# Neighbourhood attention: the two end half blocks of keys as one stacked block of 128 rows

## The chip, the cores and the metric

One core of a Trainium2 chip runs the whole kernel. The metric is the time of one execution on the device in microseconds (us); the time before is 2090.88 us, the median of three runs (2089.56 to 2090.99). The engines are called PE (TensorE, matmul), PEld (its weight load), DVE (VectorE), ACT (ScalarE), POOL (GpSimd) and SP (SyncE, which issues the transfers).

## The reference, cut to what matters

The kernel computes one inference step of a two-layer backbone for 128 context tokens and 512 latent tokens. The latent tokens form a grid of 8 rows and 64 columns. The changed part is the attention of the odd layer for the latent tokens, eight heads of width 128. Each query reads all 8 grid rows, but only a window of 16 columns, and all 128 cached context keys:

```python
s_nb = einsum('brqhd,brkwhd->brhqkw', qg, kg) * scale      # qg: queries, kg: keys of the neighbourhood
s_nb = where(col_ok, s_nb + bias, NEG)                      # learned bias by offset, NEG outside the window
s_ctx = einsum('brqhd,blhd->brhql', qg, ck) * scale         # cached context keys
p = softmax(concatenate([s_nb, s_ctx], -1), -1)
o = einsum('brhqkw,brkwhd->brqhd', pn, vg) + einsum('brhql,blhd->brqhd', pc, cv)
```

`pn` and `pc` are the two parts of `p`. Context tokens attend among themselves without a window. All of it is in 32-bit floats.

## The kernel before, in words

The projections of both layers are long streams of matmuls with 128 x 128 weight blocks. Each weight is split into a high part (`whi`, by ACT) and a low part (`wlo`, by POOL), and each activation into `acth` and `actl`, so that three fast passes (320 or 322 columns) stand for one in full precision. The odd layer's projections are done in pairs of chunks by a Strassen scheme (`spair`), whose combined weights DVE makes.

The attention heads are coroutines that run between those matmuls. The whole program is written out by a planner: class `Pace` (line 53) keeps a modelled clock for each engine, and with it the time at which each piece of a buffer becomes ready. Between two products of the weight stream `tick` lets the waiting coroutines go on, if their inputs are ready by the model (`until`, `bank`, `calm`). So the order of instructions on every engine is fixed at build time, and it follows from the modelled costs. On the chip an engine works through its own list in order; semaphores hold it back where an operand isn't there yet.

`na_head` (line 2056) is one head. The latent tokens are reordered so that eight groups of 8 columns follow one another, each of them with its 8 rows: 64 positions a group, 512 in all. The queries go in four blocks of 128 (two groups each), and a fifth block holds the context tokens' queries. The keys that the four blocks need, with the window of 16 columns, are cut at `edges` into five pieces: 64, 128, 128, 128 and 64 positions. Query block b reads pieces b and b + 1, so the first and the last half piece serve one block each (0 and 3), and each of the three full pieces serves two.

A head goes as follows.

1. The values are transposed by PE to have positions in rows: the context's 128 and the three full pieces into one PSUM bank, copied by ACT to `vk[:, 0:512]`; then the two half pieces (64 rows each) into a second bank, copied by one ACT instruction to `vk[:64, 512:768]`.
2. `blocks` (line 1662) runs the five query blocks in a software pipeline of three steps. `s1` multiplies queries with keys and adds the bias (DVE) and takes the exponential (ACT). `soft2` divides by the sum (DVE). `s3` transposes the probabilities (PE, three transposes for a latent block: two pieces and the context) and copies them from PSUM to `pT`: two DVE copies of 128 columns for the pieces, and one ACT copy for the context. A half piece has 64 rows there.
3. The final product sums everything into one bank `po` of 512 columns, in one accumulation group: the context part (128 contraction rows, 512 columns), the first half piece (64 rows, 128 columns), the three full pieces (128 rows, 256 columns each), the last half piece (64 rows, 128 columns). ACT copies `po` to the head's output rows, and a transfer takes them to DRAM.

All matmuls and transposes of a head are in 32-bit floats; one of them shows as two passes in the trace. The buffers `bm`, `vk`, `pT`, `nk` and four `pieces` lie in the memory of `Y`, which held the gating branch's normalised values until then; `open_na` (line 2538) lays them out when that branch's last products have been put in order before it.

Of the kernel before, what the change touches and what calls it, by code (L numbers as in the profile page):

```python
# [13 lines left out]
AF = mybir.ActivationFunctionType  # L14
# [227 lines left out]
class Trunk:  # L242
# [1813 lines left out]
    def na_head(self, h, q, k, vt):  # L2056
        nc, L = self.nc, self.L
        Yh = vt
        kl, ql, vl = k[:, NCTX:T], q[:, NCTX:T], vt[:, NCTX:T]
        if h:  # L2060
            yield from self.wait(f"nh{h - 1}")
        bm, nk = L["bm"], L["nk"].next()
        self.dma(bm, self.d["na_bias"][h])
        self.dma(nk[:, 0:128], self.d["cache_na_kT"][h])
        self.dma(nk[:, 128:256], self.d["cache_na_v"][h])

        spec = [(0, 3, 0), (1, 4, 320), (3, 4, 320), (5, 3, 704)]

        vk = L["vk"]
        edges = [(0, 64), (64, 192), (192, 320), (320, 448), (448, 512)]  # L2070
        yield from self.until(vt)
        pv = self.sm()
        self.tr(pv[:, 0:128], vt[:, 0:NCTX])
        for i in (1, 2, 3):
            a, e = edges[i]
            self.tr(pv[:, 128 * i : 128 * i + 128], vl[:, a:e])
        nc.scalar.activation(vk[:, 0:512], pv, AF.Copy)
        pv = self.sm()
        for i, t in ((0, 0), (1, 4)):
            a, e = edges[t]  # L2080
            self.tr(pv[:64, 128 * i : 128 * i + 128], vl[:, a:e])
        nc.scalar.activation(vk[:64, 512:768], pv[:64, 0:256], AF.Copy)
        vkt = [vk[:64, 512:640], vk[:, 128:256], vk[:, 256:384], vk[:, 384:512], vk[:64, 640:768]]
        self.flags.add(f"nv{h}")
        yield from self.until(bm, nk)
        pT = L["pT"]

        slot = {(0, 0): 768, (0, 1): 0, (1, 1): 128, (1, 2): 256, (2, 2): 384, (2, 3): 512, (3, 3): 640, (3, 4): 896}
        info = {}

        def s1(t, p):
            info[t] = p
            ps = self.sm()
            if t == 0:
                self.mm(ps[:, 0:128], q[:, 0:NCTX], k[:, 0:NCTX])
                return self.soft1(p, ps, bm[:, 192:320], 128, None)
            g0, n, off = spec[t - 1]
            n *= 64
            qs = ql[:, 128 * (t - 1) : 128 * t]
            self.mm(ps[:, 0:n], qs, kl[:, 64 * g0 : 64 * g0 + n])  # L2100
            self.mm(ps[:, n : n + 128], qs, nk[:, 0:128])
            return self.soft1(p, ps, bm[:, off : off + n + 128], n + 128, None)

        def s3(t):
            p = info[t]
            pt = self.sm()
            if t == 0:
                self.tr(pt[:, 0:128], p[:, 0:128])
                nc.vector.tensor_copy(p[:, 128:256], pt[:, 0:128])
                return  # L2110
            b = t - 1
            g0, n, off = spec[b]
            n *= 64
            for i, j in enumerate((b, b + 1)):
                a, e = edges[j]
                self.tr(pt[: e - a, 128 + 128 * i : 256 + 128 * i], p[:, a - 64 * g0 : e - 64 * g0])
            self.tr(pt[:, 0:128], p[:, n : n + 128])
            for i, j in enumerate((b, b + 1)):
                m = edges[j][1] - edges[j][0]
                s = slot[(b, j)]  # L2120
                nc.vector.tensor_copy(pT[:m, s : s + 128], pt[:m, 128 + 128 * i : 256 + 128 * i])
            nc.scalar.activation(pT[:, 1024 + 128 * b : 1152 + 128 * b], pt[:, 0:128], AF.Copy)
            if t == 1:
                po = self.sm()
                self.mm(po[:, 0:128], vk[:, 0:128], info[0][:, 128:256])
                nc.scalar.activation(Yh[:, 0:NCTX], po[:, 0:128], AF.Copy)

        yield from self.blocks(5, s1, s3, 2, ())
        self.flags.add(f"nq{h}")
        yield from self.until(pT)  # L2130
        po = self.sm()
        self.mm(po, nk[:, 128:256], pT[:, 1024:1536], stop=False)
        self.mm(po[:, 0:128], vkt[0], pT[:64, 768:896], start=False, stop=False)
        for j in (1, 2, 3):
            self.mm(po[:, 128 * (j - 1) : 128 * (j + 1)], vkt[j], pT[:, 256 * (j - 1) : 256 * j], start=False, stop=False)
        self.mm(po[:, 384:512], vkt[4], pT[:64, 896:1024], start=False, stop=True)
        y4 = Yh[:, NCTX:T].rearrange("p (r g c) -> p g r c", g=8, c=8)
        o4 = po.rearrange("p (g r c) -> p g r c", r=8, c=8)
        nc.scalar.activation(y4, o4, AF.Copy)
        self.dma(self.ysp[:, h, :], vt)  # L2140
        self.flags.add(f"nh{h}")
        yield
# [54 lines left out]
    def program(self):  # L2197
        nc, tc, d, Y = self.nc, self.tc, self.d, self.Y
# [95 lines left out]
        for h in range(4):  # L2294
# [18 lines left out]
            p = (f"gla_elem{h - 1}",) if h else ()  # L2313
# [57 lines left out]
        for kv in range(2):  # L2371
# [26 lines left out]
            for h in range(4 * kv, 4 * kv + 4):  # L2398
                if kv and h != 5:
                    i = max(h - 5, 0)  # L2400
# [137 lines left out]
        def open_na():  # L2538
            S = self.slots
            L["hq"], L["hk"], L["nv"] = (Ring([S[n] for n in x]) for x in ("AB", "CD", "ER"))  # L2540
            more = Y.rearrange("p a b -> p (a b)")
            at = [0]

            def yt(n):
                at[0] += n
                return more[:, at[0] - n : at[0]]

            L["bm"], L["vk"], L["pT"] = yt(1024), yt(768), yt(1536)
            L["nk"] = Ring([yt(256), self.wraws[:, 1792:2048]])
            self.pieces = [yt(384) for _ in range(4)]  # L2550

        do(open_na)
        for h in range(8):

# [61 lines left out]
        r = acts.pop()  # L2616
# [271 lines left out]
```

## Time and profile before

| | |
|---|---|
| median of three runs | 2090.88 us |
| the profiled execution, its own time | 2094.82 us |
| its span, first to last instruction | 2093.0 us |
| instructions in the span | 40200 |
| PE, PEld busy | 98%, 95% |
| DVE, ACT, POOL busy | 63%, 51%, 61% |
| mean granted TensorE clock | 0.996 |

The span is what the trace covers; the profiled execution's own time has a little around it. "Busy" counts the records of an engine, and PE's records overlap, since a matmul begins while the one before it is still draining; a full PE is therefore not the same as a PE at its best pace. The helpers that record every instruction for the planner have one line for all of them (L215 for DVE, ACT and POOL, L400 for matmuls, L405 for transposes), so groups are told apart by the buffers they write and read, and by form. "128*128 128x256" is a matmul with a stationary block of 128 rows and 128 columns, and a moving operand of 128 rows and 256 columns.

### The profile page before, as it was taken

The numbers are of one execution on the slowest core, as the hardware profiler recorded it, in microseconds if no ns is written. First come the engines' busy times: TensorE is split into PE (matmuls) and PEld (weight loads), VectorE is DVE, ScalarE is ACT, GpSimd is POOL, SyncE is SP. The second block draws the span as 40 slices with busy tenths as digits, with TensorE's granted clock in tenths as the row PEclk, the third lists the DMA queues.
The fourth block names the chain that finished last, engine by engine and source line by source line (L and its number), as shares of the span: only waits on it lengthen the run. The fifth ranks groups of instructions, "written<-read, shape, count | busy, mean of one in ns | idle before, by whom it ended". The sixth has DMA issues, their size and how long they took to land. (4 is left out here: it accounts for less than half of the span.)

```text
span 2093.0 us, 40200 instructions
## 1 busy us (share of the span) xinstructions
PE 2047.3 (98%) x14345; PEld 1995.9 (95%) x14345; DVE 1327.3 (63%) x3070; ACT 1064.4 (51%) x2446; POOL 1275.1 (61%) x1072
## 2 busy tenths in 40 slices
PE   7999999999999999999999999999999999999997
PEld 6889999999999999999999999999999999999997
DVE  4757677676555655788786878787454554456444
ACT  5545555445665765444564434444444554454443
POOL 4655454445545554788765666655555577768884
PEclk9999999999999999999999999999999999999998
DMA  9956333436456444577734454454322334363427
GB/s 367 396 195 205 124 122 110 142 112 188 153 170 190 142 137 148 167 222 226 249 131 135 136 159 153 139 156 139 98 86 95 95 129 135 112 235 121 139 90 251
DMA packets 192697, 340.18 MB, mean 163 GB/s; under 512 B 20752, under 2 KB 70000, under 8 KB 192496
## 3 DMA queue, kind: packets, MB, share of 16 engines
q1 hardware_dynamic: 191296, 336.45, 49.7%
q8 instruction: 112, 1.84, 0.4%
q10 hardware_dynamic: 1200, 1.17, 0.2%
q14 instruction: 89, 0.73, 0.1%
HBM read 303.03 MB, written 31.88 MB: 160 GB/s over the span
## 5 line engine op out<-in xcount | busy, mean ns | idle before, releaser
L400 PE MATMUL bank<-acth,whi 128*128 128x320 f32 (+3 forms) x3320 | 1017.7, 317 | 4.7 <-ACT YB L215 1.4
L400 PE MATMUL bank<-acth,wlo 128*128 128x320 f32 (+3 forms) x3320 | 991.7, 310 | 0.9 <-POOL wlo L215 0.9
L400 PE MATMUL bank<-actl,whi 128*128 128x320 f32 (+3 forms) x3320 | 991.5, 310 | 0.0
L215 POOL TENSOR_TENSOR wlo<-wraw,whi 128x512 fp32r<-128x512 f32 (+1 forms) x446 | 568.1, 1285 | 439.1 <-ACT whi L215 368.4
L400 PEld LDWEIGHTS bank<-acth,whi 128*128 128x128 f32 (+1 forms) x3320 | 614.9, 188 | 12.5 <-issue 3.0
L400 PEld LDWEIGHTS bank<-actl,whi 128*128 128x128 f32 (+1 forms) x3320 | 615.5, 188 | 1.7
L400 PEld LDWEIGHTS bank<-acth,wlo 128*128 128x128 f32 (+1 forms) x3320 | 614.1, 188 | 1.9 <-POOL wlo L215 1.9
L215 POOL TENSOR_TENSOR wlo<-rs,whi 128x384 fp32r<-128x384 f32 x370 | 407.9, 1120 | 205.6 <-ACT whi L215 173.2
L215 ACT ACTIVATE whi<-wraw 128x512 fp32r<-128x512 f32 (+1 forms) x456 | 261.3, 588 | 126.7 <-PE bank L400 85.7
L215 ACT ACTIVATE whi<-rs 128x384 fp32r<-128x384 f32 x370 | 184.4, 518 | 83.2 <-PE bank L400 69.1
L400 PE MATMUL bank<-eh,whi 128*128 128x322 f32 (+1 forms) x666 | 208.9, 314 | 1.0 <-ACT whi L215 1.0
L400 PE MATMUL bank<-eh,wlo 128*128 128x322 f32 (+1 forms) x666 | 206.8, 310 | 1.2 <-POOL wlo L215 0.9
L400 PE MATMUL bank<-el,whi 128*128 128x322 f32 (+1 forms) x666 | 206.3, 310 | 0.0
L215 DVE CUSTOM_DVE_ANT_0 adas<-adas,bank,partg 128x256 bf16<-128x256 f32 (+1 forms) x296 | 160.6, 543 | 15.6 <-DMA adas<-ada_g 8.0
L215 DVE TENSOR_TENSOR wraw<-rs 128x768 f32<-128x768 f32 x74 | 98.8, 1335 | 100.7 <-DMA rs<-w_odd 55.4
L215 POOL TENSOR_TENSOR prod<-adas,mixrow 128x512 f32<-128x512 f32 x76 | 99.4, 1317 | 68.5 <-ACT prod L215 47.9
L215 ACT ACTIVATE arena<-arena,bc 128x512 f32<-128x512 f32 (+4 forms) x189 | 97.8, 538 | 78.6 <-DVE arena L215 73.7
L400 PEld LDWEIGHTS bank<-eh,wlo 128*128 128x128 f32 x666 | 125.1, 188 | 2.4 <-POOL wlo L215 2.4
L400 PEld LDWEIGHTS bank<-eh,whi 128*128 128x128 f32 x666 | 125.4, 188 | 1.3 <-ACT whi L215 1.2
L400 PEld LDWEIGHTS bank<-el,whi 128*128 128x128 f32 x666 | 125.4, 188 | 0.0
L215 DVE CUSTOM_DVE_ANT_0 adas<-adas,bank,part 128x512 bf16<-128x512 f32 x150 | 111.6, 744 | 19.6 <-DMA adas<-ada 16.7
L215 DVE TENSOR_TENSOR bank<-bank,sums 128x320 f32<-128x320 f32 (+1 forms) x148 | 70.8, 493 | 82.5 <-PE bank L400 61.3
(226 smaller groups left out, 2458.9 us busy)
## 6 DMA issues: line engine op xcount, KB each, us to landing
wraw<-w_even SPq DMA_DIRECT2D x176, 256.0 KB, 3.4
adas<-ada_g SPq DMA_DIRECT2D x128, 256.0 KB, 3.7
adas<-ada SPq DMA_DIRECT2D x128, 256.0 KB, 3.7
rs<-w_odd SPq DMA_DIRECT2D x50, 384.0 KB, 3.3
wraw<-w_odd SPq DMA_DIRECT2D x74, 256.0 KB, 3.6
wraw<-w_out SPq DMA_DIRECT2D x60, 256.0 KB, 3.9
rs<-w_odd SPq DMA_DIRECT2D x50, 256.0 KB, 3.8
Y<-ada SPq DMA_DIRECT2D x24, 512.0 KB, 7.8
```

The source lines that it names most:

```text
L215: return f(*args, **kw)
L400: self.nc.tensor.matmul(out, lhsT, rhs, start=start, stop=stop, **kw)
```

## The change

The two half pieces are laid above each other as one block of 128 rows: the first piece's 64 rows stay in rows 0 to 63, the last piece's go to rows 64 to 127.

- Values: the first half piece is transposed as before. For the last one, 128 positions (384 to 511) are transposed, so that its 64 land in rows 64 to 127. ACT copies the two halves with two instructions into one block `vk[:, 512:640]`.
- Probabilities: the last block's transpose takes 64 columns more (`lead`), so that its half piece lands in rows 64 to 127 too, and the copy takes those rows. The other rows of the two strips of `pT` are filled with zeros once, by POOL in `open_na`.
- Copies: for the two middle query blocks, whose two pieces lie side by side in `pT`, DVE makes one copy of 256 columns in place of two of 128.
- Product: one matmul of 128 rows and 256 columns takes the place of the two of 64 rows and 128 columns. Its output is two strips of `po`, columns 0 to 127 and 384 to 511. It stands last in the group; the first half piece's product stood second.
- `vk` is 128 columns shorter, and the buffers behind it move up.

```diff
@@ na_head: values
-        for i, t in ((0, 0), (1, 4)):
-            a, e = edges[t]
-            self.tr(pv[:64, 128 * i : 128 * i + 128], vl[:, a:e])
-        nc.scalar.activation(vk[:64, 512:768], pv[:64, 0:256], AF.Copy)
-        vkt = [vk[:64, 512:640], vk[:, 128:256], vk[:, 256:384], vk[:, 384:512], vk[:64, 640:768]]
+        self.tr(pv[:64, 0:128], vl[:, 0:64])
+        self.tr(pv[:, 128:256], vl[:, 384:512])
+        nc.scalar.activation(vk[:64, 512:640], pv[:64, 0:128], AF.Copy)
+        nc.scalar.activation(vk[64:, 512:640], pv[64:, 128:256], AF.Copy)
...
+        lead = {(3, 4): 64}
@@ s3
                 a, e = edges[j]
+                a -= lead.get((b, j), 0)
                 self.tr(pt[: e - a, 128 + 128 * i : 256 + 128 * i], p[:, a - 64 * g0 : e - 64 * g0])
...
-            for i, j in enumerate((b, b + 1)):
-                m = edges[j][1] - edges[j][0]
-                s = slot[(b, j)]
-                nc.vector.tensor_copy(pT[:m, s : s + 128], pt[:m, 128 + 128 * i : 256 + 128 * i])
+            if b in (1, 2):
+                s = slot[(b, b)]
+                nc.vector.tensor_copy(pT[:, s : s + 256], pt[:, 128:384])
+            else:
+                for i, j in enumerate((b, b + 1)):
+                    o = lead.get((b, j), 0)
+                    r, s = slice(o, o + edges[j][1] - edges[j][0]), slot[(b, j)]
+                    nc.vector.tensor_copy(pT[r, s : s + 128], pt[r, 128 + 128 * i : 256 + 128 * i])
@@ final product
         self.mm(po, nk[:, 128:256], pT[:, 1024:1536], stop=False)
-        self.mm(po[:, 0:128], vkt[0], pT[:64, 768:896], start=False, stop=False)
         for j in (1, 2, 3):
-            self.mm(po[:, 128 * (j - 1) : 128 * (j + 1)], vkt[j], pT[:, 256 * (j - 1) : 256 * j], start=False, stop=False)
-        self.mm(po[:, 384:512], vkt[4], pT[:64, 896:1024], start=False, stop=True)
+            self.mm(po[:, 128 * (j - 1) : 128 * (j + 1)], vk[:, 128 * j : 128 * j + 128], pT[:, 256 * (j - 1) : 256 * j], start=False, stop=False)
+        ends = po.rearrange("p (a b) -> p a b", b=128)[:, 0:4:3, :]
+        self.mm(ends, vk[:, 512:640], pT[:, 768:1024].rearrange("p (a b) -> p a b", b=128), start=False, stop=True)
@@ open_na
-            L["bm"], L["vk"], L["pT"] = yt(1024), yt(768), yt(1536)
+            L["bm"], L["vk"], L["pT"] = yt(1024), yt(640), yt(1536)
...
+            nc.gpsimd.memset(L["pT"][64:, 768:896], 0.0)
+            nc.gpsimd.memset(L["pT"][:64, 896:1024], 0.0)
```

## The prediction

> **What bounds the kernel now.** I read the page first, then the busy time by stretches, then the chain of waits, and last the order of TensorE's instructions inside the changed stage. A word on measure: 0.2% of 2090.9 us is 4.2 us, and a difference below that can't be told from no change here.
>
> ```profile
> span 2093.0 us, 40200 instructions
> ...
> PE 2047.3 (98%) x14345; PEld 1995.9 (95%) x14345; DVE 1327.3 (63%) x3070; ACT 1064.4 (51%) x2446; POOL 1275.1 (61%) x1072
> ```
>
> TensorE (PE) is busy 98% of the span, no other engine above 63%. The changed code runs where the eight attention heads of the odd layer run, about 1330 to 1700 us. These are that stretch and the one behind it; the columns are the window, its length, then busy us and instruction counts of PE, PEld, DVE, ACT and POOL, then the granted clock and DMA:
>
> ```profile
> 1330.00:1700.00 370.00, 370.00 (x2464) 356.81 (x2463) 220.39 (x653) 181.34 (x453) 208.43 (x188) 1.00 0.37 114
> 1700.00:2050.00 350.00, 350.00 (x2381) 349.95 (x2380) 172.63 (x265) 160.20 (x349) 269.46 (x234) 1.00 0.43 139
> ```
>
> PE is busy all 370 and all 350 us, at full granted clock; the others have 40% or more free in the first stretch. The chain of waits that ended last says the same: from the end of the last head's blocks it is one unbroken run of matmuls (start, length, engine, count):
>
> ```profile
> 1681.37 387.59 PE bank L400 x2602
> ```
>
> So PE time taken out of a head is end-to-end time, as long as PE's operands stay early. But "busy" is not "streaming": the record of a matmul spans its waiting for weights as well. What a matmul costs is read from start to start.
>
> **The change, part by part.** *The final product.* These are PE's rows of one head's last product (the second head), single instructions from narrow windows of the timeline: start, length, form as rows*columns of the stationary block, then the moving one. An fp32 matmul shows as two passes.
>
> ```profile
> 1400.51 0.30 PE L400 MATMUL bank<-eh,whi 128*128 128x322 f32 x1
> ...
> 1400.95 1.02 PE L400 MATMUL bank<-Y,wraw 128*128 128x512 f32 x2
> 1401.38 0.59 PE L400 MATMUL bank<-Y,wraw 128*128 128x512 f32 x1
> 1401.91 0.37 PE L400 MATMUL bank<-Y 64*128 64x128 f32 x1
> 1402.12 0.27 PE L400 MATMUL bank<-Y 64*128 64x128 f32 x1
> 1402.32 0.48 PE L400 MATMUL bank<-Y 128*128 128x256 f32 x1
> 1402.64 0.38 PE L400 MATMUL bank<-Y 128*128 128x256 f32 x1
> 1402.86 0.38 PE L400 MATMUL bank<-Y 128*128 128x256 f32 x1
> ...
> 1403.50 0.38 PE L400 MATMUL bank<-Y 128*128 128x256 f32 x1
> 1403.81 0.37 PE L400 MATMUL bank<-Y 64*128 64x128 f32 x1
> 1404.03 0.27 PE L400 MATMUL bank<-Y 64*128 64x128 f32 x1
> 1404.23 0.41 PE L400 MATMUL bank<-acth,whi 128*128 128x322 f32 x1
> 1404.48 0.31 PE L400 MATMUL bank<-actl,whi 128*128 128x322 f32 x1
> ```
>
> The steady paces: a 512-column pass 1401.38 - 1400.95 = 0.43 us; a 256-column pass (1403.50 - 1402.64) / 4 = 0.215, four steps because three passes lie between; a 322-column weight pass (1400.95 - 1400.51) / 3 = 0.147. By column that is 0.84 ns for fp32, so 128 columns would be 0.107.
>
> The 64-row passes don't keep that pace. The 512's second pass should be through at 1401.38 + 0.43 = 1401.81, but the 64-row one starts at 1401.91: 0.10 lost. Its second pass follows after 0.21 where 0.107 would do: 0.10. The 256 comes 0.20 behind that: 0.09. The second 256 pass comes 0.32 behind the first, where 0.215 is the pace: 0.105. So one half block costs four exposed steps, about 0.40 us beside its 0.215 of streaming. The second half block, from 1403.50, repeats it: 0.31 to the first pass (0.095 lost), 0.22 (0.11), 0.20 (0.09), and 0.25 to the second weight pass (0.10). Why it is exposed stands in the weight-load rows:
>
> ```profile
> 1401.90 1.58 PEld L400 LDWEIGHTS bank<-Y 64*128 64x128 f32 x8 [0.76 <-issue]
> 1403.81 0.29 PEld L400 LDWEIGHTS bank<-Y 64*128 64x128 f32 x2 [0.33 <-DVE arena L215]
> ```
>
> The weight loader, which elsewhere runs one pass ahead of the matmuls, stood idle 0.76 and 0.33 us and loads the 64-row block only when the pass before has run out. The releaser of the second (a DVE work on another buffer) is only the last semaphore that the profile found; both places look alike, so I take it as a drain at the change of block height, not as a wait for data.
>
> Stacked, there is no 64-row pass left. The new sequence is 512 columns (2 x 0.43), then four products of 256 columns (8 x 0.215), then the weight stream. From the first 512 pass to the second weight pass it should last 0.86 + 1.72 + 0.15 = 2.73 us. Before, it lasts 1404.48 - 1400.95 = 3.53 here, and as much in the first and the last head:
>
> ```profile
> 1357.03 3.34 PE L400 MATMUL bank<-Y 128*128 128x512 f32 x12
> ...
> 1360.55 0.31 PE L400 MATMUL bank<-actl,whi 128*128 128x320 f32 x1
> 1689.23 1.02 PE L400 MATMUL bank<-Y,wraw 128*128 128x512 f32 x2
> ...
> 1692.75 0.31 PE L400 MATMUL bank<-actl,whi 128*128 128x322 f32 x1
> ```
>
> 1360.55 - 1357.03 = 3.52 and 1692.75 - 1689.23 = 3.52. Gain: 3.52 - 2.73 = 0.79 us a head. All 32 such passes (8 heads, 4 each) show it in one group of weight loads (count, busy us, mean ns, idle us before them):
>
> ```profile
> L400 PEld LDWEIGHTS bank<-Y 64*128 64x128 f32 x32 | 4.7, 184 | 8.7 <-issue 7.4 <-DVE partg L215 0.7 <-DVE arena L215 0.3
> ```
>
> So 8 x 0.79 = **6.3 us off PE**. What the trace doesn't show is a product written in two strips of one bank, 384 columns apart. From below: the pace of the contiguous 256 (0.215 a pass). From above: each of its passes pays an exposed step as the 64-row ones do, on either side, 2 x 0.105 a head more, so 0.58 a head and 4.6 us in all. I take the first, since the form (128 rows, 128 columns, 256 moving, a contiguous moving operand) is that of the three products ahead of it, which already write at different places of the same bank without loss. The zeros cost nothing of their own: the 256 columns stream either way.
>
> A rule of the Trainium skill speaks against all this. "TensorE: Matmul & The Clock Gate" says, in the table of "Why this matters for your kernels", that a product with few contraction rows takes the time of one with 128, and in "Back-to-back issue gap" it counts columns only; by that, two products of 128 columns and one of 256 cost alike, and the sum is nothing. The trace differs: 0.61 us for a half block where its columns are worth 0.215. "TensorEngine Tiling (Array Packing)", "Key Properties", has the rule that would join the two: changing the tiling mode drains the engine. The rows above look like that.
>
> *The transposes.* Two of each head's 64-wide ones become 128 wide (one of values, one of probabilities, the last block's); the count stays. A trio of the last block (full, half, context) beside a trio of full blocks:
>
> ```profile
> 1354.93 0.49 PE L405 MATMUL bank<-ident,Y 128*128 128x128 f32 x3
> 1355.17 0.39 PE L400 MATMUL bank<-acth,whi 128*128 128x320 f32 x1
> ...
> 1395.67 0.49 PE L405 MATMUL bank<-ident,Y 128*128 128x128 f32 x3
> 1395.91 0.39 PE L400 MATMUL bank<-acth,whi 128*128 128x320 f32 x1
> ```
>
> 0.24 us both: a narrow stationary block is no loss, only a low one is. Nothing on PE, from either side.
>
> *The copies and the zeros.* ACT's one copy of both halves becomes two, DVE's two copies of a middle block become one of 256 columns, POOL gets two fills of 64x128, once.
>
> ```profile
> L215 ACT ACTIVATE Y<-bank 128x128 f32<-128x128 f32 x30 | 8.3, 276 | 16.4 <-DVE Y L215 12.5 <-DVE den L215 3.5
> ...
> L215 ACT ACTIVATE Y<-bank 64x256 f32<-64x256 f32 x7 | 2.6, 367 | 0.0
> L215 DVE COPY Y<-bank 128x128 f32<-128x128 f32 x52 | 13.6, 286 | 18.0 <-PE bank L405 17.7
> L215 POOL MEMSET psum<- 128x128 f32 x4 | 0.8, 204 | 0.7 <-DVE partg L215 0.4 <-DVE partb L215 0.4
> 1247.49 1.28 PE L400 MATMUL bank<-arena,Y 128*128 128x128 f32 x10
> POOL wlo L215 <- PE bank L400: 20.9, 9, 3.0
> ```
>
> ACT: 2 x 0.276 - 0.367 = +0.19 us a head, 1.5 us in all, behind ACT's half-free stretch. Queued behind it are the splits of the next weights into their high parts (whi), for which POOL's low parts (wlo) and then PE wait. If that cover were gone it would cost PE those 1.5 us. DVE: two copies of 0.286 become one of between 0.286 and 0.572, twice a head: 0 to 0.57 us a head less, on an engine that PE doesn't wait for, so nothing. POOL: at most 2 x 0.204 us once. The fills must come behind PE's reads of the same columns by the gating products; those columns belong to the fourth and fifth of eight, and the fifth runs at 1247.49, before the heads begin at about 1330. POOL itself waits 20.9 us for PE between 1300 and 1700, that is, for ring slots that PE hasn't yet freed: it is ahead. No DMA is added; the buffers behind move by 128 columns and keep their sizes.
>
> **Sum.** -6.3 (product) + 0 + 0. Against the profiled execution's own time, 2094.82 us (span 2093.0 and 1.8 around it), this gives 2088.5. That execution lies 3.9 us above the median of the runs, so on the median it is 2090.9 - 6.3 = **2084.6 us**, 0.30% faster.
>
> **The rivals.** *Half the gain.* The strips' price from above, 4.6 us saved: 2086.3. For it: no row with such an output. Against: the three 256 products beside it.
>
> *Nothing saved.* Either columns alone count, as the cited rule has it, or the gain is given back because PE runs into its weights: 2090.9. Against the first: the lost steps sit at each 64-row pass and nowhere else in these rows. For the second: POOL waits for ACT's whi more than for anything. Against: POOL's waits for PE above, and 208 of 370 us busy.
>
> *Slower.* The order of all instructions is written out beforehand from modelled costs; every head has five softmax blocks whose transposes are put into the matmul stream where the model says that the probabilities are ready. One came too early already:
>
> ```profile
> 1398.80 0.31 PEld L405 LDWEIGHTS bank<-ident,Y 128*128 128x128 f32 x3 [0.27 <-DVE Y L215]
> ```
>
> With other costs the blocks shift against DVE and ACT, and PE reaches them earlier than before. If all 40 blocks came early by this 0.27 us, that is 10.8 us lost, less 6.3: +4.5, 2095.4. It outweighs the gain from 24 of the 40 on. For it: the margin at this place was none. Against: one such stall in all eight heads, and DVE gets less work, not more.
>
> **How the numbers follow.** 0.77 for the forecast, 0.09 for half the gain, 0.09 for nothing saved (0.05 and 0.04 for its two ways), 0.05 for slower. "Faster" needs a time below 2086.7: the forecast and some two thirds of the half gain, less a little for a shifted order: 0.82; same 0.13; slower 0.05. The forecast's own spread is the runs' (2089.56 to 2090.99) and the 0.2 us of the one stall: 2083.1 to 2085.6. The range goes down to the first and up past the half gain with the same spread: 2083.0 to 2087.6. It leaves out nothing saved and slower, 0.14.
>
> **What would show it.** Right: no 64-row form in PE's groups, 16 more passes of 128x256, 2.73 us from the 512's first pass to the second weight pass, the weight loader's 8.7 us of idle gone, the stretch of the heads some 6 us shorter, and the stretch behind it unchanged. Wrong: a 0.1 us step left around the new product (the strips), PE idle before transposes or before weight passes (the order, the supply), or a span shorter by the heads' gain but longer elsewhere.

## The result, and the profile after

The changed kernel takes 2083.98 us (median of 22 runs), the kernel before 2090.93 us (22 runs beside them). The ratio is 0.9969, with a 95% interval of 0.9961 to 0.9978: faster by 0.31%, or some 4.6 to 8.2 us. The forecast was 2084.6 us, 0.30%.

The page of the changed kernel, as far as it answers to the lines shown of before:

```profile
span 2080.2 us, 40147 instructions
...
PE 2040.6 (98%) x14329; PEld 1995.9 (96%) x14329; DVE 1328.8 (64%) x3054; ACT 1068.3 (51%) x2454; POOL 1278.0 (61%) x1074
```

PE has 16 passes less, one product of two passes in each of eight heads, and DVE 16 copies less. The span, though, is 12.8 us shorter, nearly twice the 6.95 us between the medians. To see what belongs to the change, take two instructions that every version has: the first head's first transposes, and the first sum of squares for the last norm. Before (the profile of the prediction):

```profile
1329.94 0.82 PE L405 MATMUL bank<-ident,arena 128*128 128x128 f32 x6
...
2066.79 0.81 PE L400 MATMUL bank<-arena,ones 128*128 128x384 f32 x2
```

After:

```profile
1322.95 0.82 PE L405 MATMUL bank<-ident,arena 128*128 128x128 f32 x6
...
2053.95 0.81 PE L400 MATMUL bank<-arena,ones 128*128 128x384 f32 x2
```

From the one to the other it is 736.85 us before and 731.00 after: 5.85 us less. The other 7.0 us lie ahead of the heads, where the change adds nothing but POOL's two fills. The kernel before, unchanged and profiled once more, reaches the heads about as much sooner:

> The kernel before, unchanged, profiled once more. If the 7 us by which the changed kernel's trace reaches the first head's transposes sooner come from the execution and not from the change, this trace reaches them at some other time than 1329.94 us, too, while a head's product takes 3.52 us again and the way from the first head's transposes to the last norm's sums takes 736.9 us again.

```profile
1322.48 0.82 PE L405 MATMUL bank<-ident,arena 128*128 128x128 f32 x6
...
2059.38 0.81 PE L400 MATMUL bank<-arena,ones 128*128 128x384 f32 x2
```

It reaches the first transposes at 1322.48 us, and then takes 736.90. So the execution behind the first profile of before lost its 7 us ahead of the heads, and the stretch from the heads on repeats within 0.05 us in these two traces. That makes it a finer measure than the time of a run, and the experiments use it.

The second head's final product after, single passes from narrow windows of PE's timeline:

```profile
1399.86 0.59 PE L400 MATMUL bank<-Y,wraw 128*128 128x512 f32 x1
1400.29 0.59 PE L400 MATMUL bank<-Y,wraw 128*128 128x512 f32 x1
1400.72 0.38 PE L400 MATMUL bank<-Y 128*128 128x256 f32 x1
1400.94 0.38 PE L400 MATMUL bank<-Y 128*128 128x256 f32 x1
...
1402.02 0.38 PE L400 MATMUL bank<-Y 128*128 128x256 f32 x1
...
1402.26 0.50 PE L400 MATMUL bank<-acth,whi 128*128 128x322 f32 x1
1402.60 0.31 PE L400 MATMUL bank<-actl,whi 128*128 128x322 f32 x1
```

There is no loss of 0.1 us left. From the 512-column passes on, each pass follows the one before by its own streaming, 0.43 and 0.215 us, and the stacked product in two strips keeps that pace: 1402.02 is its first pass, six steps behind 1400.72. Its second one and the first weight pass bring PE to 1402.60, 0.58 us later, which is 2 x 0.215 + 0.147. (The record of the first weight pass starts at 1402.26, only 0.03 behind the stacked product's second pass at that pace, and 0.34 ahead of the next one; so the sum over it is what counts.) From the first 512 pass to the second weight pass it takes 1402.60 - 1399.86 = 2.74 us by these rows. All eight heads lie between 2.729 and 2.738 us; before, they lay between 3.522 and 3.525. The gain is 0.79 us a head, 6.33 us in eight.

### The profile page after: what moved, and what is told of

It reads as the page before. It is cut to its first block, busy times and chain, and to the rows that moved or that the text cites. A ratio compares the mean times of both kernels' runs of the same rounds, so it can differ in the third digit from the quotient of the medians.

```text
span 2080.2 us, 40147 instructions
## 1 busy us (share of the span) xinstructions
PE 2040.6 (98%) x14329; PEld 1995.9 (96%) x14329; DVE 1328.8 (64%) x3054; ACT 1068.3 (51%) x2454; POOL 1278.0 (61%) x1074
```

## The experiments

Each of them is read by the same two measures: the length of a head's product (first 512 pass to second weight pass), and the stretch from the first transposes to the last norm. "Stay" means a run of 64-row passes with full-height ones on both sides: the kernel before has two a head. "Mode" in the expectations is a name for the state that PE is in during a stay; the traces show what going there and back costs, not what happens inside.

| kernel | stays | product, us a head | stretch, us | ratio to before (95%) |
|---|---|---|---|---|
| before | 2 | 3.52 | 736.85, 736.90 | |
| changed | 0 | 2.73 | 731.00 | 0.9969 (0.9961 to 0.9978) |
| padded to 128 rows | 0 | 2.74 | 731.23 | 0.9970 (0.9959 to 0.9981) |
| padded to 96 rows | 0 | 2.75 | 731.25 | one run, no interval |
| adjacent | 1 | 3.14 | 733.87 | 0.9986 (0.9977 to 0.9995) |
| twice the passes | 2 | 3.86 | 739.57 | 1.001 (1.000 to 1.002) |
| four stays | 4 | 4.54 | 744.95 | 1.0033 (1.0022 to 1.0044) |
| copies put back | 0 | 2.73 (one head 2.80) | 730.65 | 0.9968 (0.9950 to 0.9986) |
| side by side | 1 | 2.92 | 732.34 | one run, no interval |

**Padding alone.** The kernel before; nothing is stacked, but each half block gets rows of zeros.

```diff
-        self.mm(po[:, 0:128], vkt[0], pT[:64, 768:896], start=False, stop=False)
+        self.mm(po[:, 0:128], vkt[0], pT[:, 768:896], start=False, stop=False)
...
-        self.mm(po[:, 384:512], vkt[4], pT[:64, 896:1024], start=False, stop=True)
+        self.mm(po[:, 384:512], vkt[4], pT[:, 896:1024], start=False, stop=True)
...
+            nc.gpsimd.memset(L["pT"][64:, 768:1024], 0.0)
+            nc.gpsimd.memset(L["vk"][64:, 512:768], 0.0)
```

(`vkt[0]` and `vkt[4]` take all 128 rows too.)

> The kernel before, with its two half blocks kept as two products of 128 columns, but each padded with rows of zeros to 128 rows (two more fills, once). Theory (the gain is the height of the block: a product of 64 rows makes PE drain): the same gain as the whole change. From the 512-column pass to the second weight pass a head takes 0.86 + 6 x 0.215 + 4 x 0.107 + 0.15 = 2.73 us, and the time falls by 8 x 0.79 = 6.3 us, 0.30%. Rival (the gain is that one product with two strips takes the place of two): still 3.52 us a head and no gain. Rival (the gain is the shifted order and DVE's fewer copies): 3.52 us a head, no gain.

PE's timeline, second head; ten passes, four of 128 and six of 256 columns, merge into one row:

```profile
1392.68 1.02 PE L400 MATMUL bank<-Y,wraw 128*128 128x512 f32 x2
1393.53 1.90 PE L400 MATMUL bank<-Y 128*128 128x128 f32 x10
...
1395.42 0.31 PE L400 MATMUL bank<-actl,whi 128*128 128x322 f32 x1
```

1395.42 - 1392.68 = 2.74 us, and the ratio is the changed kernel's. The whole gain is there with as many products as before, each into its own strip, and with DVE's copies unchanged. PE's instructions stand in the same order as before, so neither that order nor the wait for DVE that the loader's row named in the prediction holds the 64-row pass back. It is the height of the blocks. That one product takes the place of two is worth the 0.01 us between 2.74 and 2.73.

**96 rows.** The same with 32 rows of zeros (`pT[:96]`, `vk[:96]`).

> As the padded kernel, but with 32 rows of zeros only, so the half blocks are 96 rows high. Theory, narrow form (only a block of 64 rows changes the mode of the array): 2.73 us a head, as with 128 rows. Rival (any block that isn't full makes PE drain): 3.52 us a head.

```profile
1392.28 1.02 PE L400 MATMUL bank<-Y,wraw 128*128 128x512 f32 x2
1393.14 1.91 PE L400 MATMUL bank<-Y 96*128 96x128 f32 x10
...
1395.03 0.31 PE L400 MATMUL bank<-actl,whi 128*128 128x322 f32 x1
```

2.75 us (of the ten passes merged here, four have 96 rows and six are the full pieces'): a block of 96 rows that isn't full loses nothing. Of the three heights run here, 64 is the one that does.

**One stay in place of two.** The kernel before with one line moved: the first half block's product goes behind the three full ones.

```diff
         self.mm(po, nk[:, 128:256], pT[:, 1024:1536], stop=False)
-        self.mm(po[:, 0:128], vkt[0], pT[:64, 768:896], start=False, stop=False)
         for j in (1, 2, 3):
...
+        self.mm(po[:, 0:128], vkt[0], pT[:64, 768:896], start=False, stop=False)
         self.mm(po[:, 384:512], vkt[4], pT[:64, 896:1024], start=False, stop=True)
```

> The kernel before, with the first half block's product moved behind the three full ones, next to the last half block's; all still 64 rows high. Theory with an exposed load at each pass of 64 rows and one drain for each change of height: two changes fewer, 0.86 + 6 x 0.215 + 0.10 + 3 x 0.213 + 0.20 + 0.25 = 3.34 us a head, 0.18 less than before, 1.4 us in all (0.07%, not to be told from nothing by the time; the trace tells). Rival (the loss belongs to each product and not to the change of height): 3.52 us.

```profile
1393.64 1.02 PE L400 MATMUL bank<-Y,wraw 128*128 128x512 f32 x2
...
1395.58 0.38 PE L400 MATMUL bank<-Y 128*128 128x256 f32 x1
1395.89 0.37 PE L400 MATMUL bank<-Y 64*128 64x128 f32 x1
1396.33 0.27 PE L400 MATMUL bank<-Y 64*128 64x128 f32 x1
1396.53 0.42 PE L400 MATMUL bank<-acth,whi 128*128 128x322 f32 x1
1396.78 0.31 PE L400 MATMUL bank<-actl,whi 128*128 128x322 f32 x1
```

3.14 us, not 3.34: the gain is 0.39 us a head, twice what was expected, and the time fell by 0.14% (3.1 us by the product, 0.15%). The expectation took each 64-row pass to wait for its weights. The four passes start at 1395.89 and, the last, at 1396.33: 0.44 us for three steps. The first step into the mode was 0.21 before, so the two others are 0.11 each, the streaming of 128 columns. Once in the stay PE keeps its pace. The loss belongs to the stay: 3.14 - 2.73 = 0.41 us for one, and (3.52 - 2.73) / 2 = 0.40 for each of two.

**Twice the passes, and four stays.** Both cut each half block's product into two of 64 columns. The first leaves the pieces where the product stood; the second puts them between the full ones (piece, full, piece, full, piece, full, piece). It is shortened here: `half` is the product of one piece of 64 columns, `full` that of one full piece.

```diff
-        self.mm(po[:, 0:128], vkt[0], pT[:64, 768:896], start=False, stop=False)
+        self.mm(po[:, 0:64], vkt[0], pT[:64, 768:832], start=False, stop=False)
+        self.mm(po[:, 64:128], vkt[0], pT[:64, 832:896], start=False, stop=False)
...
+        half(0, 0, False)
+        full(1)
+        half(0, 64, False)
+        full(2)
+        half(1, 0, False)
+        full(3)
+        half(1, 64, True)
```

> The kernel before, with each half block's product cut into two of 64 columns: the same columns and the same number of changes of height, twice as many passes of 64 rows. If each pass of 64 rows waits for its weights to load after the pass before has run out: four passes more at 0.107 us, 3.95 us a head, 3.4 us slower in all. If PE loses time only where the height changes: 3.52 us a head and the same time.

```profile
1396.87 1.02 PE L400 MATMUL bank<-Y,wraw 128*128 128x512 f32 x2
1397.83 0.32 PE L400 MATMUL bank<-Y 64*128 64x64 f32 x1
1398.21 0.27 PE L400 MATMUL bank<-Y 64*128 64x64 f32 x1
1398.41 0.48 PE L400 MATMUL bank<-Y 128*128 128x256 f32 x1
...
1400.74 0.31 PE L400 MATMUL bank<-actl,whi 128*128 128x322 f32 x1
```

Neither number came true: 3.86 us, between 3.52 and 3.95 and nearer the upper. The four passes of a stay start from 1397.83 to 1398.21: 0.38 us for three steps, 0.16 and twice 0.11, where their columns are worth 0.053 each. These passes follow no faster than at 0.11 us, so the four added ones cost 3.86 - 3.52 = 0.34 us a head, 0.085 each, and not the 0.107 of a load that nothing covers.

> The kernel before, with each half block's product cut into two of 64 columns as in the kernel with twice the passes, and these four pieces put between the full products: four changes into the 64-row mode and back where there were two. If the loss belongs to each stay in the mode (about 0.40 us of it at the way in and out), a stay of two 64-column passes lasts 0.10 + 0.16 + 0.20 + 0.105 = 0.56 us, and a head takes 0.86 + 6 x 0.215 + 4 x 0.56 + 0.15 = 4.54 us, 1.02 more than before: 8.1 us slower in all, 0.39%. Rival (it belongs to the number of passes): as with twice the passes, 3.86 us a head.

```profile
1396.93 1.02 PE L400 MATMUL bank<-Y,wraw 128*128 128x512 f32 x2
1397.88 0.32 PE L400 MATMUL bank<-Y 64*128 64x64 f32 x1
1398.04 0.27 PE L400 MATMUL bank<-Y 64*128 64x64 f32 x1
1398.24 0.48 PE L400 MATMUL bank<-Y 128*128 128x256 f32 x1
1398.56 0.38 PE L400 MATMUL bank<-Y 128*128 128x256 f32 x1
...
1401.47 0.31 PE L400 MATMUL bank<-actl,whi 128*128 128x322 f32 x1
```

4.54 us a head, as expected to 0.01, and the time rises by 0.33% (8.1 us by the product, 0.39%, within the interval). The passes are those of the kernel ahead of it; only two more stays were made of them, for 0.34 us each. Beside what its columns take at full height (2.73 us), a head loses 0, 0.41, 0.79 and 1.81 us with zero, one, two and four stays. The last is 0.45 a stay and not 0.40, because the step out of the stay takes 0.20 us behind a pass of 64 columns (1398.04 to 1398.24) as it does behind one of 128.

**Copies put back.** The changed kernel, with DVE's copies of the middle blocks as before.

```diff
-            if b in (1, 2):
-                s = slot[(b, b)]
-                nc.vector.tensor_copy(pT[:, s : s + 256], pt[:, 128:384])
-            else:
-                for i, j in enumerate((b, b + 1)):
...
+            for i, j in enumerate((b, b + 1)):
```

> The changed kernel, with DVE's copies of the middle blocks' pieces put back to two of 128 columns each. Theory (DVE is off the path): the product stays at 2.73 us a head, and the time stays the changed kernel's, 6.3 us (0.30%) below before. Rival (part of the gain is the fewer copies, or the order that follows from them): the gain shrinks by that part, at most by 16 x 0.57 = 9 us if all copies counted.

```profile
1393.50 1.02 PE L400 MATMUL bank<-Y,wraw 128*128 128x512 f32 x2
...
1396.23 0.31 PE L400 MATMUL bank<-actl,whi 128*128 128x322 f32 x1
```

2.73 us (in the third head 2.80, with one step between the 512-column passes 0.07 longer), ratio 0.9968, stretch 730.65: nothing of the gain came from the fewer copies.

**Side by side.** The Trainium skill ("TensorE: Matmul & The Clock Gate", "Part 3: Packing small matmuls") would have small blocks run at the same time in different rows of the array. The stacked layout allows it, since the second half block lies in rows 64 to 127. In this kernel the last half block's product goes to a bank of its own and isn't added to the output.

```diff
-        ends = po.rearrange("p (a b) -> p a b", b=128)[:, 0:4:3, :]
-        self.mm(ends, vk[:, 512:640], pT[:, 768:1024].rearrange("p (a b) -> p a b", b=128), start=False, stop=True)
+        self.mm(po[:, 0:128], vk[:64, 512:640], pT[:64, 768:896], start=False, stop=True)
+        p2 = self.sm()
+        self.mm(p2[:, 0:128], vk[64:, 512:640], pT[64:, 896:1024])
```

> The changed kernel, with the stacked product taken apart again: the first half block from rows 0 to 63 into the common bank, the last one from rows 64 to 127 into a bank of its own, next to each other. The last half block's product is not added to the output here, so the last query block lacks that part. Theory with no overlap of the two: as if both were 64 rows in the same place, 3.34 us a head. Rival (the two halves of the array work side by side, and only the drain into and out of the 64-row mode remains): the second one's first load is hidden, about 3.1 us. It would be better than stacking only below 2.73.

```profile
1399.36 1.02 PE L400 MATMUL bank<-Y,wraw 128*128 128x512 f32 x2
...
1401.60 0.38 PE L400 MATMUL bank<-Y 64*128 64x128 f32 x2
1401.82 0.28 PE L400 MATMUL bank<-Y 64*128 64x128 f32 x2
...
1402.28 0.30 PE L400 MATMUL bank<-actl,whi 128*128 128x322 f32 x1
```

The passes go in pairs, one of each half, that start within 0.01 us of each other: this rule of the Trainium skill is true here. It saves 0.22 us against one stay in the same rows (2.92 against 3.14), more than the expected 3.1 us would have. But the stay remains, and stacking is 0.19 us a head better, with one product and no second bank to add.

## Why the prediction was right, point by point

**What bounds the kernel.** Right. Of 6.33 us taken from PE in the heads, 5.85 arrive at the end of the stretch. Behind the heads nothing changed, as forecast: from the last head's second weight pass to the last norm it is 374.04 us before (1692.75 to 2066.79) and 374.10 after, from this row to 2053.95:

```profile
1679.85 0.31 PE L400 MATMUL bank<-actl,whi 128*128 128x322 f32 x1
```

**The final product.** 2.73 us was forecast for a head, 2.73 was measured, and the strips cost nothing: a pass of the stacked product takes the 0.215 of its neighbours. The four exposed steps around a half block were read rightly for this kernel, with its stays of two passes. Where they come from was read too simply in the expectations behind it, as the adjacent kernel shows: the second step is paid once, on the way in, not at each pass.

**The weight loader as a sign.** Half right. The prediction took the loader's idle time before the 64-row loads (8.7 us in all) for the drain's mark and expected it gone. The 64-row loads are gone, but the full-height loads of the same buffer now have more idle time, with no loss on PE. Before and after, in the stretch of the heads:

```profile
L400 PEld LDWEIGHTS bank<-Y 128*128 128x128 f32 x72 | 12.2, 189 | 1.8
...
L400 PEld LDWEIGHTS bank<-Y 128*128 128x128 f32 x88 | 15.9, 190 | 5.1 <-issue 3.8
```

The loads behind the two 512-column passes of the second head, after:

```profile
1400.29 0.19 PEld L400 LDWEIGHTS bank<-Y 128*128 128x128 f32 x1 [0.24 <-issue]
1400.72 1.49 PEld L400 LDWEIGHTS bank<-Y 128*128 128x128 f32 x7 [0.24 <-issue]
```

A loader that runs one pass ahead waits out each 512-column pass of 0.43 us: 0.24 us twice a head, 3.8 us in eight. So of 8.7 + 1.8 = 10.5 us only 5.4 went, and idle time alone is no measure of the loss. What the prediction read from the start of the load holds: now the load at 1400.29 is one pass ahead of the 256-column pass at 1400.72 that uses it, while the 64-row load started at 1401.90, together with its own pass. The size comes from the step from start to start on PE, which the sum was made of.

**Transposes, copies, zeros.** All off the path, as forecast, at these prices (groups of the changed kernel):

```profile
L215 ACT ACTIVATE Y<-bank 64x128 f32<-64x128 f32 x14 | 3.7, 266 | 0.1
...
L215 DVE COPY Y<-bank 128x256 f32<-128x256 f32 x16 | 6.8, 424 | 6.9 <-PE bank L405 6.7
1277.15 0.46 POOL L215 MEMSET Y<- 64x128 f32 x2
```

ACT pays 2 x 0.266 - 0.367 = 0.17 us a head (0.19 forecast); DVE's wide copy takes 0.424 us, between the bounds 0.286 and 0.572; POOL's two fills take 0.46 us together (at most 0.41 forecast) and run at 1277.15 without a wait.

**The rivals.** Half the gain and nothing saved fell with the rows above. With them falls the rule that only columns count (the Trainium skill, "TensorE: Matmul & The Clock Gate", "Why this matters for your kernels" and "Back-to-back issue gap"), for a 64-row product that stands alone between full ones: a half block of 128 columns takes 0.61 us at 64 rows and 0.22 at 96 or 128. Inside a stay it holds, with 0.11 us for a pass of 128 columns. The rule that a change of the tiling mode drains the engine (the Trainium skill, "TensorEngine Tiling (Array Packing)", "Key Properties") fits all the runs, with 0.40 us for a stay of 128-column passes. The slower rival's mechanism did appear, at a small price. PE lost 0.48 us (6.33 - 5.85), and the changed kernel's rows show two waits:

```profile
1345.42 0.30 PE L400 MATMUL bank<-el,whi 128*128 128x322 f32 x1
1345.93 0.19 PEld L400 LDWEIGHTS bank<-eh,wlo 128*128 128x128 f32 x1 [0.46 <-POOL wlo L215]
...
1346.18 0.31 PE L400 MATMUL bank<-eh,whi 128*128 128x322 f32 x1
...
1367.53 0.53 PEld L405 LDWEIGHTS bank<-ident,arena 128*128 128x128 f32 x5 [0.27 <-ACT arena L215]
```

In the first head the loader waited 0.46 us for a weight's low part, and before a set of transposes 0.27 us for ACT; the one stall of before, 0.27 us, is gone. By PE's own starts the first cost 0.47 us (0.76 from 1345.42 to 1346.18, where two steps of 0.147 would do), the second 0.21, and the stall of before had cost 0.22: 0.46 in all. The late low part is also there in the kernel with the halves side by side, which keeps the wide copy, and not in the one with the copies put back, though that has ACT's added copy too. So it goes with the wide copy; whether by its length or by the order that the planner made with it was not separated. A return of this size needs no wide copy, though. The kernel padded to 128 rows, with the copies and the order of before, gives back 0.6 us (6.24 off the heads, 5.65 at the end of the stretch), some 0.4 of it at one place where PE now waits for a copy by ACT:

```profile
1460.62 0.49 PE L400 MATMUL bank<-arena 128*128 128x128 f32 x2 [0.28 <-ACT Y L215]
```

**The sum.** 6.3 us forecast; 6.95 by the medians, with an interval (4.6 to 8.2) that holds 6.3; 5.85 by the stretch. That the medians came within 0.6 us of the forecast time is partly luck, with an interval that wide; that a head came within 0.01 us is not. The forecast's own spread was too narrow, and one end of it is a slip: the slowest of the three runs and the one stall give 2084.6 + 0.11 + 0.2 = 2084.9, not 2085.6. The 22 runs of before beside the result lie from 2086.29 to 2097.17, where three had shown 2089.56 to 2090.99.

## What to carry to other kernels

In these fp32 products a block of 64 rows among full ones costs some 0.4 us beside its columns each time that PE goes over to it and back. Rows of zeros up to 96 or 128 take that away without more columns, and gave the same time here as stacking two such blocks (ratios 0.9970 and 0.9969 for 128 rows and the stack); padding is the smaller edit. Where half-height blocks must stay, put them next to one another. Read PE by the steps between starts, summed over several passes, not by busy time or by the loader's idle time, and compare two traces between instructions that both have, since a trace can be 7 us off ahead of the place of the change.

## What the hardware showed beside that

- 96 rows behave as 128: no loss of 0.1 us on the way in or out (2.75 us a head against 2.74).
- Inside a stay the passes follow at 0.11 us whether they have 64 or 128 columns; only the step behind the first pass is longer (0.16 and 0.21), and the one out of the stay (0.20 for both).
- Two 64-row products in different halves of the array started within 0.01 us of each other, and the steps into the stay and out of it took as long as for one block (0.31 and 0.20 us).
